# Split-GELU multiply on one core: tile 0 moved by whole transfers, tiles 0 and 1 computed in steps of one, three and four rows

## The chip, the core and the metric

The kernel runs on one core of a Trainium2 chip. The metric is the device time of one execution in microseconds (us). Of the kernel before, three runs gave a median of 469.17 us (469.15 to 469.35).

Three engines have work here. ScalarE (ACT) computes the GELU and also issues transfers on a DMA queue of its own, q10 in the profile. VectorE (DVE) multiplies. SyncE (SP) computes nothing and issues transfers on the queue q1. The transfers of both queues are carried out by the same 16 DMA engines of the core.

## What is computed

```python
def reference(x):                       # x: 32 x 512 x 2048, float32
    half_dim = x.shape[-1] // 2
    x1, x2 = x[..., :half_dim], x[..., half_dim:]
    gelu_x1 = 0.5 * x1 * (1 + erf(x1 / np.sqrt(2)))
    return gelu_x1 * x2                 # 32 x 512 x 1024, float32
```

There are 16,384 rows of 2048 numbers. The input is 134.2 MB, the output 67.1 MB, and nothing is used twice.

## The kernel before

The rows are cut into 16 tiles (`n_tiles`). A tile has 8 consecutive rows (`R`) for each of the 128 partitions, so one partition's share of a tile is 64 KB of contiguous memory on the way in and 32 KB on the way out. A tile is 8.39 MB in and 4.19 MB out. There are two input buffers `x0_tile` and `x1_tile` and two output buffers `o0_tile` and `o1_tile`; tile i uses buffer i % 2 of each (`x_tile` and `o_tile` in the profile).

The order of the work is written out by hand, with semaphores:

- Before the loop, ACT issues a small transfer into `scrap` (the `opening`), and SP issues the loads of tile 0, in two halves of 4 rows with the semaphores `first[0]` and `first[1]`, and of tile 1, whole, with `ready[1]`. SP's queue works off its transfers in the order of issue.
- For each tile, the loop runs over steps of rows (line 79): 2, 2 and 4 rows for the first and the last tile (`pieces`), 5 and 3 for the others. Each step is one GELU on ACT (line 87), from the left half of the rows of `x_tile` into `o_tile`, and one multiplication on DVE (line 95), in place in `o_tile`, with the right half of the same rows. `gelu_done` lets DVE follow ACT, `mul_done` counts the multiplications that are done.
- The store of a tile is issued on ACT's queue (line 56) after the multiplications that it needs. Tile 0 is stored in two halves, each as soon as its 4 rows are done. Tile 14, and tile 15 in two halves, are stored on SP's queue, behind the last load.
- The load of tile i + 2 (line 49) is issued by SP when all multiplications of tile i are done, since it overwrites the input buffer of tile i.
- The semaphore `ready[k]` counts the load of tile i + 2 and the store of tile i together. The first GELU of tile i + 2 waits for both (line 85), because it overwrites the output buffer from which tile i is stored.

What ACT and SP issue is in program order on each: a store that waits for a multiplication holds up the next GELU behind it on ACT.

Of the kernel before, what the change touches and what calls it, by code (L numbers as in the profile page):

```python
# [1 line left out]

# [4 lines left out]

GELU = mybir.ActivationFunctionType.Gelu


@with_exitstack
def kernel(
    ctx: ExitStack,
    tc: tile.TileContext,
    x: bass.AP,
    out: bass.AP,
):
    nc = tc.nc
    P = nc.NUM_PARTITIONS

    x_flat = x.flatten_outer_dims()
    out_flat = out.flatten_outer_dims()
    n_rows, dim = x_flat.shape
    half = dim // 2

    R = 8
    x_t = x_flat.rearrange("(n p r) d -> n p r d", p=P, r=R)
    o_t = out_flat.rearrange("(n p r) d -> n p r d", p=P, r=R)
    n_tiles = x_t.shape[0]
    x_bufs = [nc.alloc_sbuf_tensor(f"x{k}_tile", [P, R, dim], x.dtype) for k in range(2)]  # L30
    o_bufs = [nc.alloc_sbuf_tensor(f"o{k}_tile", [P, R, half], out.dtype) for k in range(2)]

    first = [nc.alloc_semaphore(f"first{j}") for j in range(2)]
    ready = [nc.alloc_semaphore(f"ready{k}") for k in range(2)]
    gelu_done = nc.alloc_semaphore("gelu_done")
    mul_done = nc.alloc_semaphore("mul_done")
    tail_stored = nc.alloc_semaphore("tail_stored")
    opened = nc.alloc_semaphore("opened")  # L40
    scrap = nc.alloc_sbuf_tensor("scrap_tile", [8, 128], x.dtype)
    n = {sem.name: 0 for sem in [*first, *ready, gelu_done, mul_done, tail_stored, opened]}

    def counted(ins, sem, by):
        ins.then_inc(sem, by)
        n[sem.name] += by

    def load(i, rows, sem):
        ins = nc.sync.dma_start(out=x_bufs[i % 2][:, rows, :], in_=x_t[i][:, rows, :])  # L49
        counted(ins, sem, 16)  # L50
        return ins

    def store(queue, i, rows, sem):
        queue.wait_ge(mul_done, n[mul_done.name])
        counted(
            queue.dma_start(out=o_t[i][:, rows, :], in_=o_bufs[i % 2][:, rows, :]), sem, 16
        )

    opening = nc.scalar.dma_start(out=scrap[:, :], in_=x_t[0][:8, 0, :128])
    counted(opening, opened, 16)
    for ins in (
        opening,
        load(0, slice(0, 4), first[0]),
        load(0, slice(4, 8), first[1]),
        load(1, slice(0, 8), ready[1]),
    ):  # L70
        tc.no_tile_sem_insts.add(ins.ins.name)
    tc.close()
    tc.compile()  # L73

    for i in range(n_tiles):
        k = i % 2
        last = i == n_tiles - 1
        pieces = i == 0 or last
        steps = ((0, 2), (2, 4), (4, 8)) if pieces else ((0, 5), (5, 8))
        for lo, hi in steps:  # L80
            rows = slice(lo, hi)
            if i == 0 and lo % 4 == 0:
                nc.scalar.wait_ge(first[lo // 4], 16)
            elif lo == 0:
                nc.scalar.wait_ge(ready[k], n[ready[k].name])
            counted(
                nc.scalar.activation(  # L87
                    out=o_bufs[k][:, rows, :], in_=x_bufs[k][:, rows, :half], func=GELU
                ),
                gelu_done,  # L90
                1,
            )
            nc.vector.wait_ge(gelu_done, n[gelu_done.name])
            counted(
                nc.vector.tensor_mul(  # L95
                    out=o_bufs[k][:, rows, :],
                    in0=o_bufs[k][:, rows, :],
                    in1=x_bufs[k][:, rows, half:],
                ),
                mul_done,  # L100
                1,
            )
            if pieces and hi % 4 == 0:
                if last:
                    store(nc.sync, i, slice(hi - 4, hi), tail_stored)
                else:
                    store(nc.scalar, i, slice(hi - 4, hi), ready[k])
        if not pieces:
            if i == n_tiles - 2:
                store(nc.sync, i, slice(0, R), tail_stored)  # L110
            else:
                store(nc.scalar, i, slice(0, R), ready[k])
        if i + 2 < n_tiles:
            nc.sync.wait_ge(mul_done, n[mul_done.name])
            load(i + 2, slice(0, R), ready[k])


    nc.scalar.wait_ge(opened, 16)
    nc.scalar.drain()  # L119
    for sem in (*first, *ready, opened):  # L120
        nc.scalar.sem_clear(sem)
    nc.vector.drain()
    nc.vector.sem_clear(gelu_done)
    nc.sync.sem_clear(mul_done)
    nc.sync.wait_ge(tail_stored, n[tail_stored.name]).then_inc(
        tail_stored, -n[tail_stored.name]
    )


# [1 line left out]
_INS = ['x']  # L131
_OUTS = [((32, 512, 1024), 'float32')]


# [23 lines left out]
```

## Time and profile before

| | |
|---|---|
| median of three runs | 469.17 us |
| span of the profiled execution, first to last instruction | 467.8 us |
| what the median has beside that span | 1.4 us |
| DVE busy | 140.5 us (30%), 34 instructions |
| ACT busy | 115.5 us (25%) |
| DMA | 201.34 MB, 430 GB/s over the span |
| a whole load from issue to landing, median | 44.4 us |
| a whole store from ACT's queue, issue to landing, median | 44.7 us |

The profile is of one execution, and its own time is the span: the records begin with the first instruction and end with the last. The 1.4 us lie between that span and the device time that is reported. "Busy" counts instructions of an engine, not transfers. A queue's transfer is seen in three places: its issue (a short instruction on ACTq or SPq), its packets (one packet here is one partition's contiguous share, moved by one of the 16 DMA engines), and its landing, when its semaphore has been counted up and the instruction that waited for it goes on.

### The profile page before, as it was taken

To read this page: it belongs to the slowest core of one execution; us is meant where nothing else is said; L and a number is where in the kernel's file an instruction comes from. 1 tells how busy PE (TensorE), PEld (TensorE's weight loads), DVE (VectorE), ACT (ScalarE), POOL (GpSimd) and SP (SyncE) were. 2 spreads that over 40 slices of the span, in tenths; PEclk is the share of its full clock that TensorE was granted. 3 is DMA by queue.
4 is the path that set the end of the run, shared out by engine and by line. 5 is a ranking of instruction groups with operands and counts; after the bars stand their busy time and mean duration, and the time that the engine had idled before them with its cause. 6 is when DMAs were issued, how large, how long until landed. Compare 5 with 4: busy or idle time off the path is not lost.

```text
span 467.8 us, 154 instructions
## 1 busy us (share of the span) xinstructions
DVE 140.5 (30%) x34; ACT 115.5 (25%) x35; POOL 0.2 (0%) x4
## 2 busy tenths in 40 slices
DVE  0330515207051060511606115060150702507043
ACT  1320606041060410604105050050501506014060
POOL 0000000000000000000000000000000000000000
DMA  8999999999999999999999999999999999999988
GB/s 359 448 448 448 398 406 496 403 403 448 459 437 403 440 412 493 403 403 448 487 409 403 445 406 493 403 403 448 493 403 403 448 426 471 403 426 426 493 384 379
DMA packets 5057, 201.34 MB, mean 430 GB/s; under 512 B 568, under 2 KB 576, under 8 KB 576
## 3 DMA queue, kind: packets, MB, share of 16 engines
q1 hardware_dynamic: 2880, 142.61, 70.6%
q10 hardware_dynamic: 2176, 58.73, 29.1%
q14 instruction: 1, 0.01, 0.0%
HBM read 134.22 MB, written 67.11 MB: 430 GB/s over the span
## 4 chain that ended last, share of the span: by engine, by line
DMA 76%; DVE 14%; ACT 8%; ACTq 0%; SPq 0%; issue 0%
DMA out_dram<-o_tile 66%; DVE o_tile L95 14%; DMA x_tile<-in_x_dram 10%; ACT o_tile L87 8%; ACTq L119 0%; SPq L49 0%
## 5 line engine op out<-in xcount | busy, mean ns | idle before, releaser
L95 DVE TENSOR_TENSOR o_tile<-o_tile,x_tile 128x5120 f32<-128x5120 f32 (+3 forms) x34 | 140.5, 4171 | 319.7 <-ACT o_tile L87 319.7
L87 ACT ACTIVATE o_tile<-x_tile 128x5120 f32<-128x5120 f32 (+3 forms) x34 | 114.3, 3407 | 337.3 <-DMA out_dram<-o_tile 301.8
L87 ACT ACT_TABLE_LOAD x1 | 1.3, 1283 | 2.9 <-PEq L73 2.9
L142 POOL MEMSET const-bfloat16-1.0<- 128x1 bf16 x1 | 0.1, 102 | 0.0
L142 POOL MEMSET const-uint8-127<- 128x1 uint8 x1 | 0.1, 101 | 0.0
L142 POOL MEMSET const-float32-0.0<- 128x1 f32 x1 | 0.1, 99 | 0.2 <-issue 0.2
L142 POOL MEMSET const-float32-1.0<- 128x1 f32 x1 | 0.1, 98 | 0.0
## 6 DMA issues: line engine op xcount, KB each, us to landing
out_dram<-o_tile ACTq DMA_DIRECT2D x13, 4096.0 KB, 44.7
x_tile<-in_x_dram SPq DMA_DIRECT2D x2, 4096.0 KB, 16.7
out_dram<-o_tile ACTq DMA_DIRECT2D x2, 2048.0 KB, 34.4
out_dram<-o_tile SPq DMA_DIRECT2D x1, 4096.0 KB, 25.2
out_dram<-o_tile SPq DMA_DIRECT2D x2, 2048.0 KB, 7.8
x_tile<-in_x_dram SPq DMA_DIRECT2D x15, 44.4
scrap_tile<-in_x_dram ACTq DMA_DIRECT2D x1, 4.0 KB
```

The lines of the kernel that those rows point to most:

```text
L87: nc.scalar.activation(out=o_bufs[k][:, rows, :], in_=x_bufs[k][:, rows, :half], func=GELU),
L95: nc.vector.tensor_mul(out=o_bufs[k][:, rows, :], in0=o_bufs[k][:, rows, :], in1=x_bufs[k][:, rows, half:],),
L142: nc = _bacc.Bacc("TRN2", target_bir_lowering=False, num_devices=1)
```

## The change

Tile 0 is loaded by one transfer of 8 rows, on `ready[0]`, and stored by one transfer of 8 rows; `first` is gone. Tiles 0 and 1 are computed in steps of one, three and four rows. Tile 15 keeps its steps of 2, 2 and 4 rows and its two stores, and tiles 2 to 14 keep their steps of 5 and 3. ACT now has 3 instead of 2 GELUs for tile 1, and DVE 3 instead of 2 multiplications. The line numbers shift: line 49 becomes 48, 56 becomes 55, 87 becomes 86, and 95 becomes 94.

```diff
-    first = [nc.alloc_semaphore(f"first{j}") for j in range(2)]
     ready = [nc.alloc_semaphore(f"ready{k}") for k in range(2)]
...
         opening,
-        load(0, slice(0, 4), first[0]),
-        load(0, slice(4, 8), first[1]),
+        load(0, slice(0, 8), ready[0]),
         load(1, slice(0, 8), ready[1]),
...
-        pieces = i == 0 or last
-        steps = ((0, 2), (2, 4), (4, 8)) if pieces else ((0, 5), (5, 8))
+        pieces = last
+        if i < 2:
+            steps = ((0, 1), (1, 4), (4, 8))
+        else:
+            steps = ((0, 2), (2, 4), (4, 8)) if last else ((0, 5), (5, 8))
         for lo, hi in steps:
             rows = slice(lo, hi)
-            if i == 0 and lo % 4 == 0:
-                nc.scalar.wait_ge(first[lo // 4], 16)
-            elif lo == 0:
+            if lo == 0:
                 nc.scalar.wait_ge(ready[k], n[ready[k].name])
...
             if pieces and hi % 4 == 0:
-                if last:
-                    store(nc.sync, i, slice(hi - 4, hi), tail_stored)
-                else:
-                    store(nc.scalar, i, slice(hi - 4, hi), ready[k])
+                store(nc.sync, i, slice(hi - 4, hi), tail_stored)
...
-    for sem in (*first, *ready, opened):
+    for sem in (*ready, opened):
         nc.scalar.sem_clear(sem)
```

More of the change, by code (lines that the diff above doesn't have):

```diff
@@ L41 @@
     scrap = nc.alloc_sbuf_tensor("scrap_tile", [8, 128], x.dtype)
-    n = {sem.name: 0 for sem in [*first, *ready, gelu_done, mul_done, tail_stored, opened]}
+    n = {sem.name: 0 for sem in [*ready, gelu_done, mul_done, tail_stored, opened]}
     def counted(ins, sem, by):
```

## The prediction

> **What bounds the kernel now.** I read the page first (span, busy shares, the DMA line), then the chain of waits, then busy time by stretches, and last the timeline of the opening and of the end. Of the page, the head, the busiest engine, and parts 2 and 3:
>
> ```profile
> span 467.8 us, 154 instructions
> DVE 140.5 (30%) x34; ACT 115.5 (25%) x35; POOL 0.2 (0%) x4
> ...
> DMA  8999999999999999999999999999999999999988
> ...
> DMA packets 5057, 201.34 MB, mean 430 GB/s; under 512 B 568, under 2 KB 576, under 8 KB 576
> ...
> q1 hardware_dynamic: 2880, 142.61, 70.6%
> q10 hardware_dynamic: 2176, 58.73, 29.1%
> ```
>
> The reader is to see that no compute engine is busy for a third of the time, while the two queues' shares add to 99.7%: the 16 DMA engines are full. Busy time by stretches (DVE and ACT busy, then TensorE's clock, DMA share, GB/s) says where they are not:
>
> ```profile
> 22.50:47.00 24.50, 4.42 (x1) 3.59 (x1) 0.00 (x0) 1.00 0.99 428
> 71.40:100.40 29.00, 8.76 (x2) 7.12 (x2) 0.00 (x0) 1.00 1.00 434
> 100.40:448.50 348.10, 105.13 (x24) 85.47 (x24) 0.00 (x0) 1.00 1.00 432
> 448.50:467.80 19.30, 8.92 (x3) 7.21 (x3) 0.00 (x0) 1.00 0.95 408
> ```
>
> The share is 0.99 to 1.00 until the last load has landed at 448.5, and 0.95 behind that, with the final landing in it. The chain of waits (start, length, what) goes through transfers:
>
> ```profile
> 1.64 45.36 DMA x_tile<-in_x_dram
> 46.99 0.02 issue
> 47.02 4.48 ACT o_tile L87
> 51.50 0.02 issue
> 51.52 8.77 DVE o_tile L95 x2
> 60.29 0.02 issue
> 60.31 40.07 DMA out_dram<-o_tile
> ```
>
> It names ACT and DVE for 13.25 us of every second tile, but the DMA engines are full in those stretches too (the load of the other buffer is still in the queue), so a shorter computation moves an issue and not a byte. The time is the bytes by the packet rate. From the packet records of the trace: a packet of 65,536 bytes took 2.418 us, of 32,768 bytes 1.213, of 16,384 bytes 0.611 (medians). One of the 16 engines carries 8 packets of each transfer: 15 whole loads 15 x 8 x 2.418 = 290.2; tile 0's two half loads 16 x 1.213 = 19.4; its two half stores 16 x 0.611 = 9.8; 14 whole stores 14 x 8 x 1.213 = 135.9; the two last half stores 9.8. Sum 465.0 us. The first data packets begin at 1.7 to 2.3 us, and the last semaphore is counted up 0.4 us behind the last data. That fills the span of 467.8; there is no idle time of any size to be won or to be filled.
>
> **The change part by part.** The opening in the timeline of before:
>
> ```profile
> 12.79 3.71 ACT L87 ACTIVATE o_tile<-x_tile 128x2048 f32<-128x2048 f32 x2 [8.65 <-DMA x_tile<-in_x_dram]
> ...
> 19.26 0.38 ACTq L56 DMA_DIRECT2D out_dram<-o_tile  x1
> 22.47 3.62 ACT L87 ACTIVATE o_tile<-x_tile 128x4096 f32<-128x4096 f32 x1 [5.97 <-DMA x_tile<-in_x_dram]
> ...
> 30.58 0.36 ACTq L56 DMA_DIRECT2D out_dram<-o_tile  x1
> ```
>
> *One load in place of two.* The same bytes in packets twice as large: 8 x 2.418 - 16 x 1.213 = -0.06 us on each engine, and one semaphore write of 0.009 us less. One issue less on SP (0.42 us), hidden: load 1 is issued before 2 us and its turn is at 22. Not shown anywhere is a 64 KB packet as the very first. The first 32 KB packets took 1.63 to 2.06 us where the later ones took 1.21, an extra of 0.4 to 0.85. If that is a latency, it stays what it is, 0; if it goes with the size, it doubles, +0.85 at most. Against that, load 1's first 64 KB packets, behind 32 KB ones, took 2.50 to 2.87, up to 0.45 more than 2.418, and this can go. Ends -0.45 and +0.85; I take 0, for the extra goes from 0.42 to 0.85 at one packet size, as a start-up latency would.
>
> *One store in place of two.* 8 x 1.213 - 16 x 0.611 = -0.07 us, one semaphore write less, and one issue less on ACT (0.36 us, hidden: ACT then waits for load 1).
>
> *Tile 0's work begins and ends later.* Its first GELU goes from 12.8 to the landing of the whole load, 22.4. Durations by shape, from the groups of instructions:
>
> ```profile
> L95 DVE TENSOR_TENSOR o_tile<-o_tile,x_tile 128x3072 f32<-128x3072 f32 x14 | 46.9, 3351 | 0.0
> L87 ACT ACTIVATE o_tile<-x_tile 128x3072 f32<-128x3072 f32 x14 | 38.5, 2747 | 0.0
> L87 ACT ACTIVATE o_tile<-x_tile 128x2048 f32<-128x2048 f32 x4 | 7.4, 1901 | 30.6 <-DMA out_dram<-o_tile 21.9 <-DMA x_tile<-in_x_dram 8.7
> L95 DVE TENSOR_TENSOR o_tile<-o_tile,x_tile 128x4096 f32<-128x4096 f32 x2 | 8.8, 4424 | 7.7 <-ACT o_tile L87 7.7
> L87 ACT ACTIVATE o_tile<-x_tile 128x4096 f32<-128x4096 f32 x2 | 7.2, 3608 | 6.0 <-DMA x_tile<-in_x_dram 6.0
> ```
>
> A row more costs ACT 2.747 - 1.901 = 0.85, so one row is an estimated 1.05 us. ACT is the later of the two: 1.05 + 2.75 + 3.61, then DVE's last four rows 4.42, together 11.8. Tile 0 is done at 34.2 (before: 30.6). Store 0 waits for that on ACT, with nothing but tile 1's GELU behind it, which waits for load 1 anyway; load 2 waits on SP with nothing behind it. This costs nothing as long as load 1 covers it: its 8 packets run from 22.0 to 22.0 + 8 x 2.42 = 41.4, alone now, and load 2 has to be in the queue by then. The margin is 41.4 - 34.2 - 1.0 (issue to first packet, as at the start: 0.73 to 1.74) = 6.2 us. Without that cover the delay of 3.6 us would show.
>
> *Tile 1 in three steps.* 11.8 us after its landing it is done, against 4.47 + 8.77 = 13.25 before, though it has one instruction more on ACT and on DVE. Load 1 lands earlier (some 43 against 47.0, since fewer stores run beside it), so load 3 and store 1 are issued at about 55 instead of 60.3. Load 2 is then in SP's queue until about 71, so this is a reserve and no gain: 0.
>
> *The rest.* The two queues take turns packet by packet (in the packet records from 24 us on, one of q1, one of q10). In before they arrive together: load 15 and store 13 both at 448.5. Store 0 now enters at 36 to 41 us, with one or two packets done or none before load 1 ends, so the stores stay level with the loads or a packet or two ahead. The end keeps its form. Behind load 15 lie store 14 (8 x 1.213 = 9.7) and the first half store (4.9), 14.6 us for the engines; the last half store was issued 11.7 us after the GELU's wait ended (460.2), and would start some 1.0 later: 12.7. Cover 1.9 us from load 15, 1.3 counted in the trace (issue 460.2, first byte 462.5). Two semaphore clears fewer on ACT lie inside it.
>
> Sum: -0.06 - 0.07 - 0.02 = -0.15 us against the profiled 467.8, a span of 467.65. Around the span lie 1.37 us up to the median, which is kept: 469.17 - 0.15 = 469.02.
>
> **The rivals.**
>
> *A, slower: load 2 comes late.* If the queue doesn't hold load 1 until tile 0 is done, the 3.6 us by which load 2 is later go to the end: 469.2 + 3.6 = 472.8. It decides from the point where tile 0 ends after 40.4. For it: in the chain the first tile's load is the only thing at work until 12.8, and now until 22.4. Against it: 6.2 us of cover, and a share of 0.99 in the stretch 22.5 to 47. The Trainium skill (Perfetto Trace Analysis, DMA Optimizations) says that splitting transfers may let the task end sooner where the DMA engines are generally idle. By that condition, met nowhere here (share 0.99 to 1.00), merging loses nothing.
>
> *B, slower: the stores fall behind the loads.* Then tile 15 waits for store 13, and store 14 is partly done in that time, so that less is left to cover the last steps. Each packet of lag costs 1.2 us; one fits in the 1.3, two end at 470.3, three at 471.5. It needs a first packet of store 0 later than about 48, 14 us after the issue; in before the first half store was issued at 19.26 and its first packet ran at 24.4, 5.1 us later.
>
> *C, faster: a transfer has a price of its own on the queue.* The first half landed 12.0 us after its issue, 2.3 more than the 9.66 that its bytes take. If each transfer paid that, one load less gives 466.9, and the store may give as much again. Against it: the second half landed 9.7 us after the first (12.79, 22.47), which is its bytes alone, so transfers in a queue pay nothing. The Trainium skill (DMA: Bandwidth & Descriptors, Anatomy of one DMA — SWDGE (gpsimd) path) fits about 2.0 us plus the bytes to each DMA, for those issued from gpsimd; by that the estimate would be 467.2. The two landings here disagree.
>
> *D, slower: the opening packet.* Beyond its bound, with a whole 64 KB packet lost before the flow starts (2.4 - 1.2 = 1.2 us): 470.2.
>
> **How the numbers follow.** 0.2% (0.94 us) is about what a measurement of this kernel can tell from no change. Forecast 0.85; A 0.03, B 0.04, D 0.03, so slower 0.10; C 0.03 and 0.02 for a gain that I don't see, so faster 0.05. The range takes the ends of the opening packet, 469.02 - 0.45 and + 0.85, and the runs' spread of 0.2 about it: 468.4 to 470.0. It leaves A, B, most of D and C outside, with some 0.14.
>
> **What would show it.** Right: a span of 467.4 to 468.3, DMA share 0.99 or more in each stretch from 22 to 448, first GELU near 22.4, tile 0's store issued near 34, load 3 near 55, the last load landing between 447.5 and 448.7, and 19.3 us from there to the end. Wrong: a first GELU after 23 (D); a hole in the DMA share between 41 and 45 (A); a last GELU group that waits for a store 2 us or more after load 15's landing, and a hole before the last half store (B); a flow that ends over 1 us sooner with the same share (C).

## The result and the profile after

The changed kernel took 470.36 us (median of 15 runs, 469.73 to 471.02), the kernel before 469.25 (15 runs, 469.10 to 469.37). The ratio is 1.0021, with a 95% interval of 1.0014 to 1.0027: 1.1 us slower, 0.36 us beyond the upper end of the range, and on the side to which the prediction had given 0.10. The runs also scatter more, over 1.3 us in place of 0.3.

The profiled execution has a span of 469.0 us, 1.2 more than before. The head of its page and parts 2 and 3:

```profile
span 469.0 us, 152 instructions
DVE 140.8 (30%) x35; ACT 115.5 (25%) x36; POOL 0.2 (0%) x4
...
DMA  8999999999999999999999999999999999999998
...
DMA packets 4769, 201.34 MB, mean 429 GB/s; under 512 B 536, under 2 KB 544, under 8 KB 544
...
q1 hardware_dynamic: 2736, 142.61, 70.6%
q10 hardware_dynamic: 2032, 58.73, 29.0%
```

The same bytes go in fewer packets, the engines are as full, and yet it takes longer. Busy time by stretches (the stretches of before, the last one longer):

```profile
22.50:47.00 24.50, 9.01 (x3) 8.17 (x4) 0.00 (x0) 1.00 0.96 393
71.40:100.40 29.00, 8.76 (x2) 7.12 (x2) 0.00 (x0) 1.00 1.00 434
100.40:448.50 348.10, 105.13 (x24) 85.47 (x24) 0.00 (x0) 1.00 1.00 433
448.50:469.00 20.50, 8.92 (x3) 7.22 (x3) 0.00 (x0) 1.00 0.92 395
```

The reader is to see the first line: 393 GB/s between 22.5 and 47 us, where before had 428. Part of that comes back in the stretch behind it (47 to 71.4 us: 438 against 430), so the size of the loss is better read from the packets below. From 71 us on the flow is that of before. The timeline of the opening:

```profile
22.70 7.22 ACT L86 ACTIVATE o_tile<-x_tile 128x1024 f32<-128x1024 f32 x3 [19.05 <-DMA x_tile<-in_x_dram]
...
34.41 0.38 ACTq L55 DMA_DIRECT2D out_dram<-o_tile  x1
46.05 7.22 ACT L86 ACTIVATE o_tile<-x_tile 128x1024 f32<-128x1024 f32 x3 [16.13 <-DMA x_tile<-in_x_dram]
...
57.76 0.36 ACTq L55 DMA_DIRECT2D out_dram<-o_tile  x1
```

Tile 0 is done and its store is issued at 34.4, 0.2 us after the forecast. Load 1 lands at 46.0, where 43 was expected. The last GELU group of before and of after, from the two timelines:

```profile
448.51 7.21 ACT L87 ACTIVATE o_tile<-x_tile 128x2048 f32<-128x2048 f32 x3 [21.91 <-DMA out_dram<-o_tile]
```

```profile
449.58 7.22 ACT L86 ACTIVATE o_tile<-x_tile 128x2048 f32<-128x2048 f32 x3 [19.42 <-DMA out_dram<-o_tile]
```

In both kernels all 16 loads and stores 0 to 13 are done at that moment. It comes 1.07 us later, and behind it lie 19.4 us, 19.3 before. The row of after names a store as what ended the wait, but by the semaphore counts in the trace store 13 had landed at 446.5 and load 15 landed at 449.56: the GELU waited for the load. In before both landed at 448.5. The middle runs at a pace of 29.0 us for a tile in both (tile 3 starts at 100.40 and 104.05, tile 14 at 419.47 and 423.04). The 3.6 us between these starts are not all loss, since only 1.07 are left where the same transfers are done in both. So the loss is made ahead of 104 us, and the packet records show where. Each line is one DMA engine (L load, S store, KB of the packet, its start in us, and behind + the ns that it took beyond the median of its size), first one of before, then two of the changed kernel:

```
L32@20.56 L64@21.78+447 S16@24.64 L64@25.25 S16@27.67          (before; the 16 engines: 0 to 447 ns)
L64@36.30 L64@38.71+1096 S32@42.22 S32@43.44 L64@44.65        (changed: 10 of 16 engines about like this)
L64@36.46+708 S32@39.59 L64@40.80+1004 S32@44.21 S32@45.44 L64@46.65   (changed: 6 engines like this)
```

In the changed kernel the load packet ahead of the first store packet is held up, by about 1.1 us; on six engines, where the store comes one packet earlier, two load packets are, by 1.6 us together. Over the 16 engines that is 1.3 us each. Before had a small form of it, which I had taken for something else: its first half store began at 24.4 us, and the load packets ahead of it took 0.25 us more on the mean, later ones 0.16 more together. The last semaphore writes of the 16 engines stand at 466.9 to 467.4 (mean 467.10) in before and at 467.6 to 468.6 (mean 468.05) in after: 0.95 later on the mean, and the slowest engine, one of the six, 1.28.

### The profile page after: what moved, and what is told of

Read it like the earlier page. It is cut to its first block, busy times and chain, and to the rows that moved or that the text cites. A ratio compares the mean times of both kernels' runs of the same rounds, so it can differ in the third digit from the quotient of the medians.

```text
span 469.0 us, 152 instructions
## 1 busy us (share of the span) xinstructions
DVE 140.8 (30%) x35; ACT 115.5 (25%) x36; POOL 0.2 (0%) x4
## 4 chain that ended last, share of the span: by engine, by line
DMA 76%; DVE 13%; ACT 8%; ACTq 0%; issue 0%; SPq 0%
DMA out_dram<-o_tile 66%; DVE o_tile L94 13%; DMA x_tile<-in_x_dram 10%; ACT o_tile L86 8%; ACTq L115 0%; SPq L48 0%
## 5 line engine op out<-in xcount | busy, mean ns | idle before, releaser
L94 DVE TENSOR_TENSOR o_tile<-o_tile,x_tile 128x3072 f32<-128x3072 f32 (+4 forms) x35 | 140.8, 4057 | 320.4 <-ACT o_tile L86 320.1
L86 ACT ACTIVATE o_tile<-x_tile 128x3072 f32<-128x3072 f32 (+4 forms) x35 | 114.2, 3315 | 338.9 <-DMA out_dram<-o_tile 303.7
```

The source lines that it names most:

```text
L86: nc.scalar.activation(out=o_bufs[k][:, rows, :], in_=x_bufs[k][:, rows, :half], func=GELU),
L94: nc.vector.tensor_mul(out=o_bufs[k][:, rows, :], in0=o_bufs[k][:, rows, :], in1=x_bufs[k][:, rows, half:],),
```

## The experiments

In this part, "hold-up" is the time that load packets took beyond the median of their size, summed over the 16 engines and divided by 16. It is counted from the packet records of the profiled execution, apart from the opening packets. In the diffs, `...` stands for lines left out, the allocation of helper tiles and semaphores and the widened definition of `store` among them, and what stands behind `#` are notes.

| run | tile 0's store: packets, first packet | hold-up there, us | time, us |
|---|---|---|---|
| before | 2 x 16 KB, 24.4 | 0.25, then 0.16 | 469.25 |
| changed kernel | 32 KB, 39.6 to 42.5 | 1.3 | 470.36 |
| before, steps of tile 1 only | 2 x 16 KB, 24.5 | 0.38, then 0.22 | 469.20 |
| before, whole store only | 32 KB, 37.2 to 37.6 | 1.04 | 470.71 |
| before, both half stores late | 2 x 16 KB, 34.5 to 37.0 | 0.50, then 0.7 | 473.67 |
| changed, half stores at 34.3 | 2 x 16 KB, 39.0 to 42.5 | 0.24, then 1.03 | 474.48 |
| changed, half stores at 29.7 and 34.2 | 2 x 16 KB, 34.1 | 0.26, then 0.60 | 471.81 |
| changed, load 2 later by 2.4 us | 32 KB, 39.5 to 42.7 | 1.5 | 470.25 |
| changed, load 2 later by 4.7 us | 32 KB, 39.8 to 42.6 | 1.03, then 0.05 | 470.25 |
| changed, row 0 stored ahead | 4 KB from 29.0, 28 KB from 50.3 to 53.8 | 0.10; 0.74, then 0.39 | 472.27 |
| changed, load 1 in halves | 32 KB, 39.6 to 41.5 | 1.0 | 470.12 |
| changed, one more load | 32 KB, 39.4 to 42.7 | 0.80 | 479.83 |

**One part at a time.** First the steps of tile 1 alone, and the whole store of tile 0 alone, each on the kernel before:

```diff
         steps = ((0, 2), (2, 4), (4, 8)) if pieces else ((0, 5), (5, 8))
+        if i == 1:
+            steps = ((0, 1), (1, 4), (4, 8))
```

> The kernel before, with tile 1 alone computed in steps of 1, 3 and 4 rows: load 3 is issued some 1.4 us earlier and finds load 2 still in the queue. All theories: 469.2, no change. If the steps carry the loss: 470.3.

469.20 us, ratio 1.000 (0.9991 to 1.0008). Load 3 was issued at 59.0, 1.3 earlier, and nothing came of it: the steps of tile 1 cost and give nothing. Store 0 is the same here as in before, and the hold-up is 0.60 in place of 0.41: by so much the count can differ from one execution to another.

```diff
-                else:
-                    store(nc.scalar, i, slice(hi - 4, hi), ready[k])
+                elif hi == R:
+                    store(nc.scalar, i, slice(0, R), ready[k])
```

> The kernel before, with its two half loads and its steps of 2, 2 and 4, but tile 0 is stored by one transfer, issued at 30.6 us together with load 2. Theories SIZE and RUN: load packets of load 1 at 33 to 40 us take some 1.3 us more on each engine, time 470.2 to 470.4. Rival LOAD: as before, 469.2.

470.71 us, ratio 1.0026 (1.0016 to 1.0035): the whole store alone is enough for the loss. Its stretch shows it, with the columns as above:

```profile
22.50:47.00 24.50, 4.42 (x1) 4.03 (x2) 0.00 (x0) 1.00 0.96 399
```

All 16 engines are alike here: the sixth packet of load 1 starts at 33.7 to 34.1, takes 1.0 us more, and the store's first packet follows at 37.2 to 37.6. The first 64 KB packets of load 1, at 21.9 us behind the same 32 KB packets as in before, take no longer than the others. So what they took more in before belonged to the store behind them and not to the change of size. The eleven runs fall into two groups, five at 469.5 to 469.9 and six at 470.7 to 471.5. The profiled one took 469.87 and is of the lower group: 0.6 us above before, which is what its hold-up gives (1.04 less 0.41). What the upper ones had more was not seen.

The whole load of tile 0 was not tried alone, but the packet records bound its price. The first packet of load 1 starts (mean of the 16 engines) at 21.90 to 21.98 us in the ten profiled executions with the whole load, and at 21.87 to 21.90 in the four with two half loads. That is less than 0.1 us, so rival LOAD falls.

**Size or lateness.** In the changed kernel the whole store was cut again into two halves, first both at 34.3 us:

```diff
+            elif i == 0:
+                store(nc.scalar, i, slice(0, 4), ready[k])
+                store(nc.scalar, i, slice(4, R), ready[k])
             else:
                 store(nc.scalar, i, slice(0, R), ready[k])
```

> The changed kernel, but tile 0 is stored by two transfers of 4 rows (16 KB packets), both issued where the whole store was (34.4 us). In the changed kernel's packet records the load packets around 36 to 41 us, just ahead of the first store packets, took 1.3 us more than usual on each engine (mean of 16), against 0.25 at the first store of before. Theory SIZE (the hold-up is that of a first store packet and goes with its size): some 0.4 to 0.65 us in place of 1.3, time 469.5. Rival RUN (any store that breaks into a run of 64 KB loads holds it up, of whatever size): 1.3 us again, 470.4. Rival LOAD (the extra time comes from the whole load, not from the store): 470.4, and no difference in the packets around 36 us explains it.

474.48 us, ratio 1.012 (1.0104 to 1.0136): no theory had that. The profiled execution took 476.32, the other three 474.3 to 474.5. Load 1's seventh packet, on 12 of the 16 engines the one ahead of the first store, lost only 0.24 us, but its last one lost 1.03, so the sum did not fall. The rest of the loss is of another kind:

```profile
88.78 7.12 ACT L86 ACTIVATE o_tile<-x_tile 128x5120 f32<-128x5120 f32 x2 [37.07 <-DMA out_dram<-o_tile]
93.28 8.76 DVE L94 TENSOR_TENSOR o_tile<-o_tile,x_tile 128x5120 f32<-128x5120 f32 x2 [37.12 <-ACT o_tile L86]
102.08 0.36 ACTq L55 DMA_DIRECT2D out_dram<-o_tile  x1
```

Tile 2's GELU waits for store 0 until 88.8. The store's 16 packets on each engine have only one turn between two load packets, so they need 16 turns where load 2 has 8, and they started late. Meanwhile loads 2 and 3 run out, nothing is queued on SP, and load 4 is issued at 102 only: the packet records show 2.6 us without any packet (mean of the engines) between 100 and 104 us, and another 0.7 at 462 to 464. When loads set in again at 103 us, beside stores, their first packets are held up by another 1.4 us. This is the lag of the stores that rival B of the prediction describes, but it bites at tile 2 already and not only at tile 15. The Trainium skill (DMA: Bandwidth & Descriptors, Queues, rings and completion order) says that an engine takes turns between its queue rows packet by packet. The trace agrees, with one q1 and one q10 packet in turn, and a turn moves 16 KB here where it could move 32.

Then the first half as soon as its rows were done, by itself:

```diff
+            elif i == 0:
+                store(nc.scalar, i, slice(0, 4), ready[k], 2)   # waits for 2 multiplications
+                store(nc.scalar, i, slice(4, R), ready[k])
```

> The changed kernel, but tile 0 is stored by two transfers of 4 rows, the first issued at 29.9 us (4 rows done) by itself, the second at 34.4 with load 2. SIZE: 0.4 to 0.65 us at the first store, 469.5. RUN: 1.3 us, now at 32 to 37 us, 470.4. Rival TOGETHER (the hold-up is that of a store and a load that are issued at the same moment): no hold-up at the first store, 469.1 to 469.3.

471.81 us, ratio 1.0064 (1.005 to 1.0078). At the first store the hold-up is 0.26, as in before, though the store enters 10 us later and into a run of 64 KB packets: so lateness by itself is not what makes the first hold-up large. But the last packet of load 1 (40.9 us) lost 0.56 more, and the stores fall behind again. Stretches near the end:

```profile
440.00:456.00 16.00, 2.73 (x2) 4.67 (x3) 0.00 (x0) 1.00 0.99 426
456.00:462.00 6.00, 5.19 (x2) 2.54 (x1) 0.00 (x0) 1.00 0.82 350
```

Here the share of 0.82 is the hole that rival B describes: tile 15 waited for store 13 until 451.3, and when its first half store came, the engines had run dry 0.8 us before.

The cleanest pair for the size is the kernel before with its half stores both at 30.6 us, against the one with the whole store at 30.5:

```diff
-                else:
-                    store(nc.scalar, i, slice(hi - 4, hi), ready[k])
+                elif hi == R:
+                    store(nc.scalar, i, slice(0, 4), ready[k])
+                    store(nc.scalar, i, slice(4, R), ready[k])
```

> The kernel before with its two half loads, but both half stores of tile 0 are issued when all 8 rows are done (30.6 us). Against the run with the one whole store at 30.6 us (1.04 us more in the load packets ahead of the first store packets, on all 16 engines) only the size of the store's packets differs, 16 in place of 32 KB. Theory SIZE (the first store packet that enters a run of loads holds the load packet ahead of it until the store packet has been fetched, and a larger one takes longer): 0.25 to 0.3 us. Rival ENTRY (entering that late costs 1.0 whatever the size): 1.0 us. For the time both expect a loss of another kind: 16 turns of stores that begin some 5 turns later than before end 3 to 4 turns behind load 2, so tile 15 waits for store 13 and the engines stand idle some 1.5 us near the end: 470.5 to 471.5.

At the first store 0.50 us against 1.04, so in this pair half the packet, half the hold-up. The size does not fix it alone: the other runs with 16 KB packets have 0.24 to 0.38 there. And 0.7 more followed, most of it (0.53) at the last packet of load 1. The sum is no smaller than with 32 KB packets. 473.67 us is the median of seven runs that scatter from 469.66 to 478.31, ratio 1.0068 (1.0041 to 1.0094), and the profiled one (473.81) has a hole again, larger than expected:

```profile
456.00:462.00 6.00, 5.06 (x3) 5.40 (x3) 0.00 (x0) 1.00 0.36 156
```

**Issued together?** Store 0 and load 2 are issued within 10 ns. Load 2 was set off by two or, in a second run, four multiplications into a tile that nothing reads (the second time in bfloat16):

```diff
+            if i == 0:
+                for j in range(2):                      # range(4) in the second run
+                    nc.vector.wait_ge(mul_done, 3)
+                    nc.vector.tensor_mul(
+                        out=pad[:, j, :], in0=o_bufs[0][:, j, :], in1=o_bufs[0][:, j, :]
+                    ).then_inc(padded, 1)
+                nc.sync.wait_ge(padded, 2)              # 4
             nc.sync.wait_ge(mul_done, n[mul_done.name])
             load(i + 2, slice(0, R), ready[k])
```

> The changed kernel, but load 2 is issued some 2.5 us after store 0 (SP waits for two multiplications of one row each into a tile that nothing reads). Store 0 is then issued by itself onto ACT's queue, which is empty. Theory TOGETHER (a store that is issued onto an empty queue at the same moment as a load costs some 1.0 us more): the load packets ahead of the first store packets take 0.25 us more in place of 1.3 on each engine, time 469.2 to 469.5. Rival ENTRY (a 32 KB store onto an empty queue costs 1.0 to 1.3 us whenever it comes, and the 0.26 at the first half store of the run with the early half stores was due to its 16 KB): 1.0 to 1.3 us again, 470.3.

470.25 us, ratio 1.002 (1.0011 to 1.0029), and 1.5 us of hold-up with store 0 issued by itself at 34.50 and load 2 at 36.90. TOGETHER falls.

A mirror of it was to set off the store by a GELU ahead of it on ACT:

```diff
+                if i == 0:
+                    nc.scalar.wait_ge(mul_done, 3)
+                    nc.scalar.activation(out=pad[:, :, :], in_=o_bufs[0][:, 0:2, :], func=GELU)
                 store(nc.scalar, i, slice(0, R), ready[k])
```

> The changed kernel, but store 0 is issued some 2 us after load 2 (ACT does a GELU of two rows into a tile that nothing reads before it). TOGETHER: 0.25 us at the first store packets, some 0.05 at load 2's issue; time 469.2 to 469.5, if the stores do not fall a turn behind (then 0.5 more). ENTRY: 1.0 to 1.3 us again, 470.3 or more.

This changed nothing that it meant to. ACT issues a transfer without waiting for the GELU ahead of it to end:

```profile
34.39 1.91 ACT L111 ACTIVATE pad_tile<-o_tile 128x2048 f32<-128x2048 f32 x1 [4.49 <-DVE o_tile L95]
34.40 0.38 ACTq L56 DMA_DIRECT2D out_dram<-o_tile  x1
```

So it repeats the changed kernel: 1.44 us of hold-up, 470.40 us, ratio 1.0022 (1.0013 to 1.0031). Nine engines are held up twice in it, in place of six.

**A small store ahead, and other cuts.**

```diff
+            if i == 0 and lo == 1:
+                store(nc.scalar, i, slice(0, 1), ready[k], 1)   # row 0, at 25 us
...
-                store(nc.scalar, i, slice(0, R), ready[k])
+                store(nc.scalar, i, slice(1 if i == 0 else 0, R), ready[k])
```

> The changed kernel, but row 0 of tile 0 is stored by a transfer of its own (4 KB packets) as soon as it is done, at 25 us, and rows 1 to 7 at 34.4 together with load 2. When load 2 and the second store are issued together, ACT's queue is at work. TOGETHER: 0.1 to 0.25 us at the first store, little at 36 to 41 us. ENTRY: 0.25 us or less at the first store (small packets), nothing later. Both: the 16 turns of the two stores last three turns beyond load 2, so the first GELU of tile 2 waits for store 0 some 5 to 10 us after load 2 has landed, and what is lost there and at the end is 1 to 2 us: 470 to 471.

The 4 KB packets cost next to nothing (0.03, and 0.06 at load 1's last packet), but when the 28 KB packets followed, from 50.3 us on, the load packets ahead of them lost 0.74 and then 0.39. ACT's queue had been at work for 18 us by then, so an empty queue is not needed for a hold-up. Nor does every first large store packet bring one. In before the first 32 KB store packets (store 1) come behind the 16 KB ones at 72.9 to 73.3 us, and no load packet from 62 to 82 us took more than 0.05 us beyond the median; the same step costs nothing with the steps of tile 1 only, with both half stores late and with the halves at 29.7 and 34.2. What is shown is that 32 KB packets straight into a run of loads, and 28 KB ones behind 4 KB ones, hold it up, and 32 KB ones behind 16 KB ones do not. 472.27 us, ratio 1.0063 (1.0051 to 1.0076), above the 470 to 471 expected, with 2.1 us without packets at 458 to 462.

The store was also cut by partitions, 16 first (in two halves) and 112 behind:

```diff
+            elif i == 0:
+                store(nc.scalar, i, slice(0, 4), ready[k], slice(0, 16))    # partitions 0 to 15
+                store(nc.scalar, i, slice(4, R), ready[k], slice(0, 16))
+                store(nc.scalar, i, slice(0, R), ready[k], slice(16, P))
```

> The changed kernel, but the whole store of tile 0 is cut by partitions: partitions 0 to 15 first, in two transfers of 4 rows (one packet of 16 KB for each engine and transfer), then partitions 16 to 127 whole (7 packets of 32 KB). 9 turns in place of 8, issued at 34.4 as before. SIZE: the first store packets cost 0.25 us in place of 0.7 to 1.3; what the last packet of load 1 costs more (0.6 to 1.0 on 6 engines of the changed kernel) may stay. Time 469.4 to 469.9. ENTRY: 1.0 to 1.3, time 470.3.

485.63 us, ratio 1.035 (1.0337 to 1.0364). It says nothing on the question: load packets were held up in every tile to the end, 12.3 us for each engine with the opening against 2.0 in the changed kernel, and the stretch from 100.4 to 448.5 ran at 421 GB/s. What a cut by partitions does to the engines was not followed up.

```diff
-        load(1, slice(0, 8), ready[1]),
+        load(1, slice(0, 4), ready[1]),
+        load(1, slice(4, 8), ready[1]),
```

> The changed kernel, but load 1 is issued as two halves (32 KB packets, 16 for each engine). Theory FETCH (a 32 KB store packet is ready some 3.4 us after the load packet ahead of it began, so a shorter load packet hides less of that): 3.4 - 1.2 = 2.2 us at the first store packets, time 471. Rival FIXED (the entry of a 32 KB store packet costs 1.0 us whatever runs ahead of it): 1.0 to 1.3, time 470.3. A cost that falls with the load packets' size (0.5 or less, time 469.5) speaks against both.

1.0 us at the entry, 470.12 us, ratio 1.0018 (1.001 to 1.0027). With 32 KB load packets ahead the entry costs the same as with 64 KB: FETCH falls, in the form that the load packet hides part of it, and FIXED holds.

**The second hold-up.** One load more behind load 1, so that load 2's turn comes later (9.7 us of transfer are added):

```diff
+    def extra():   # rows 0 to 3 of tile 1, into the output buffer that tile 1's GELU overwrites later
+        ins = nc.sync.dma_start(
+            out=o_bufs[1][:, :, :].rearrange("p (r two) d -> p r (two d)", two=2),
+            in_=x_t[1][:, 0:4, :],
+        )
+        counted(ins, ready[1], 16)
+        return ins
...
         load(1, slice(0, 8), ready[1]),
+        extra(),
```

> The changed kernel with one more load of 4.19 MB (rows 0 to 3 of tile 1 into the output buffer of tile 1, which is overwritten later), issued behind load 1 at the start, so that the queue is some 9.7 us longer when load 2 is issued and load 2 comes to its turn at 51 us and not at 41. The result is the reference's; 9.7 us of transfer are added. Theory LEAD (two hold-ups: the first store packet has to be fetched, 1.0 us for 32 KB, and load 2's first packet holds up what is ahead of it when it was issued less than some 10 us before its turn): 1.0 us at the first store packets on all 16 engines, none at the last packet of load 1 or at the turn of load 2; time 479.0 to 479.7 (470.4 + 9.7 less some 0.5 to 1.0). Rival BOUNDARY (the last packet of load 1 is held up whatever is behind it): 1.6 to 1.7 us on the engines where a store packet comes one packet earlier, as in the changed kernel; 480 or more.

0.80 us at the first store, nothing at the last packet of load 1 on the 15 engines where the two can be told apart. 479.83 us, 0.1 us above the range that LEAD gave; 470.36 + 9.7 would be 480.1. By its packets LEAD held here. The other end, load 2 issued at 39.05, close to its turn:

> The changed kernel, but load 2 is issued some 4.8 us later than store 0, at 39.2 us, 2 us or less before its turn (in the run with 2.4 us it was 36.9, and the last packet of load 1 was held up by up to 1.4 us beyond the 0.7 of the changed kernel). LEAD: 2 us or more at the last packet of load 1 or as idle time behind it, time 471 to 472.5. Rival BOUNDARY: 1.3 to 1.7 us per engine as in the changed kernel, 470.3.

1.03 us at the first store and 0.05 behind it, no idle time, 470.25 us, ratio 1.0016 (1.0007 to 1.0025). LEAD expected 2 us or more and falls; BOUNDARY, which wanted the second hold-up always, falls too.

## Why the prediction was wrong

- The step that failed is the one under "The rest", that store 0 "enters at 36 to 41 us" and the end keeps its form, with no price for the entering itself. It was costed at 0. Measured: it entered at 39.6 to 42.5 us, and the load packets ahead of it were held up, 1.3 us for each engine in the changed kernel against 0.4 in before. With one whole store and nothing else changed, the median goes from 469.2 to 470.7; of these 1.5 us the profiled execution, at 469.87, shows 0.6 in its packets.
- The evidence was in the trace of before, and the step on the load misread it. Load 1's first packets took up to 0.45 us more (on one of the 16 engines nothing, so the 2.50 that the prediction gives as the least is 2.42). I put that to the change from 32 to 64 KB and made it the lower end of the range. It sat ahead of the first store packet, at 24.4 us, and the run with the whole store alone shows those packets without it. The size of the store packet was the term to ask for: the first hold-up was 0.24 to 0.50 us for 16 KB, 1.04 for 32 KB with the whole store, 0.74 for 28 KB and next to nothing for 4 KB in the run with row 0 ahead. What goes on in a DMA engine at that moment, no record here shows.
- The sum for the engines is then -0.15 (fewer packets, as predicted) + 0.9 (1.3 less 0.4) + 0.06 (opening) = +0.8; the mean of their last semaphore writes moved by 0.95. The slowest engine moved by 1.28, since six engines were held up twice. That the number of such engines changes from run to run might explain the scatter of the runs. This is argued, not shown, and the one repeat speaks little for it: nine such engines and 470.41 us, against six and 470.36.
- The opening packet was right. The first 64 KB packets took 0.65 us more than the median, the first 32 KB packets 0.59. The bound of 0.85 and rival D were not needed. That D's 470.2 lies near the result is luck, since the loss has another cause.
- Tile 0's cover was right: load 2 was issued at 34.4, load 1's last packets ended at 42 to 44.5, and the queue was never empty. Rival A did not come. The Trainium skill's condition (Perfetto Trace Analysis, DMA Optimizations: splitting may help where the DMA engines are generally idle) was not met here, at a share of 0.99 to 1.00 in before. What the prediction drew from that, that merging loses nothing, was wrong: the engines were full, and the merged kernel took 0.2% more.
- The steps of tile 1 were right at 0 (469.20). Load 3 was issued at 57.8 and not at 55, since load 1 landed later.
- The end was right in its length and not in its form. From the last GELU to the end it took 19.4 us as before, but store 13 landed 3 us ahead of load 15, and load 15 landed at 449.56, outside the 447.5 to 448.7 that were to show the prediction right. So rival B did not decide in the changed kernel. It decided in each of the four runs in which tile 0's store took 16 turns and started late, at 1.1 to 3.6 us of idle engines, so its mechanism was right, though it had no place in this change.
- Rival C's gain was not there: with two transfers fewer the kernel is slower, and the sum above needs no such term.

What stays open is the second hold-up. It came at the last packet of load 1 when load 2 had been issued at 34.2 to 36.9 (on some engines or all), and with 16 KB stores also when it had been issued at 30.6. It did not come with load 2 at 39.05, nor with one more load in the queue, nor with load 1 in halves, nor with the whole store at 30.5, and with 4 KB store packets it was 0.06. Neither its distance from load 2's issue nor the boundary alone explains that. The time hardly depends on it: with 1.08 us of hold-up in all, the run with load 2 at 39.05 is at 470.25, 0.1 below the changed kernel. No version here beats the kernel before.

## What to carry to other kernels

Where the DMA engines are full, an edit that leaves bytes and order alone can still cost at the point where a second stream begins: a first store of 16 KB packets, entered early, cost 0.4 to 0.6 us here, a whole one 0.8 to 1.5. Of the forms tried, 16 KB packets that enter early, with 32 KB ones behind them, cost least; 4 KB packets ahead only moved the cost to the 28 KB ones. And a stream that is cut small and enters late falls behind, because the two queues take turns by packets, until something waits for it. And where a few packets take longer than their size, look at what comes next on the same engine before putting it to the packet itself.

## What was not expected of the hardware

- A load packet of 64 KB, 2.42 us in all of the steady part, took 3.4 to 3.5 us just ahead of the first 32 KB store packet, on all 16 engines (run with the whole store alone). From then on the two streams interleaved without loss.
- Halves in place of one store, at the same moment, cost 4 us more (474.48 against 470.36), through turns, waits and hold-ups, not through bytes.
- The first 32 KB store packets cost the loads nothing where they came behind 16 KB ones (72.9 us in before), and 1.04 us where they came first.
- A cut of one single store by partitions (16 and 112) slowed every later tile: 421 GB/s in place of 433 for the rest of the run, 485.63 us.
- A transfer on ACT's queue was issued 0.01 us after the start of a GELU of 1.9 us that stands ahead of it in the program (34.39 and 34.40).
